# A feed-forward chunk's seven products: from five PSUM tiles to three banks, with five sums instead of seven

## The chip, the cores and the metric

The kernel runs on 1 core of one Trainium2 chip. The metric is device time in microseconds: the median of 3 runs, from the first to the last instruction of the program as the runs are timed.

## The reference

A block of a diffusion model, two layers deep, on one sequence of 512 tokens (1024 channels) with 256 context tokens. Each layer is: a feed-forward, four mixers side by side (attention in a window, a state space, grouped attention, neighbourhood attention), and a second feed-forward. Each of the three has a modulation before and after it and a norm behind it; in the last layer the context is dropped after the mixers. What the change touches is the feed-forward's first half:

```python
def swiglu(h, w_in, w_out):
    a, u = jnp.split(h @ w_in, 2, axis=-1)
    return (jax.nn.silu(a) * u) @ w_out
```

`h` has 768 tokens (512 and the context's 256) in three of the four feed-forwards and 512 in the last; `w_in` is 1024 x 5632, so that gate `a` and up `u` have 2816 columns each. All is float32.

## The kernel before, in words

**Arithmetic.** TensorE multiplies in a 32-bit format with a short mantissa (`float32r`). So each operand is split into two such parts, high and low, and `mm3` (L326 to L331) makes three matmuls of a product of two operands: high by high, low by high, high by low. A weight tile of 128 x 512 is split by `split_slot` (L322 a cast on ACT, L323 a subtraction on DVE), into one of six slots for `wh` and six for `wl`.

**Stages.** The program runs: input and modulations, feed-forward 1 of layer 0, mixers of layer 0 and their merge, feed-forward 2 of layer 0, feed-forward 1 of layer 1, mixers of layer 1 and their merge, feed-forward 2 of layer 1. A feed-forward takes its 2816 columns in 22 chunks of 128, in four to six parts; after each part the part's columns are multiplied with `w_out` and added to the residual (`branch_out`, with L468 and L470 on DVE reading and adding the sums; the last part has a form of its own). The first two chunks of each feed-forward are computed plainly (`first`), the other 20 by `winograd`, so it is called 80 times: 60 times with halves of 384 tokens, 20 times with halves of 256.

**A chunk.** Tokens and channels are halved, which makes a product of 2 x 2 blocks: A11, A12 (the first tokens) and A21, A22 (the second); B11 and B21 the gate's weights, B12 and B22 the up's. Winograd's scheme has seven block products in place of eight, with sums S1 to S4 of A's blocks, made once for each feed-forward, and T1 to T4 of B's, made for each chunk on POOL (`ffn_weights`, L605 to L613). With C11 and C21 the gate's results and C12 and C22 the up's:

```
U = A11 B11 + S2 T2      C11 = A11 B11 + A12 B21     C12 = U + S4 B22 + S1 T1
C21 = U + S3 T3 + A22 T4                             C22 = U + S3 T3 + S1 T1
```

Each block product is 4 channel chunks x 3 matmuls = 12 matmuls into one PSUM bank. `winograd` allots, for each chunk, three tiles of one bank (`psp`, two buffers) for A11 B11, A12 B21 and S1 T1, and two tiles of two banks (`ps2`, two buffers) for the others, in the order `one[:, 0]`, `two[:, 0]`, `one[:, 1]`, `two[:, 1]`. ACT copies the first product (L686); DVE adds each of the others to a running sum in SBUF (L688, L691, L692, L695, L696, L699, L700); ACT takes the silus (L689, L697), DVE multiplies (L701, L702), and `store` splits the result for the second half (L642 on ACT, L643 on DVE).

**Order.** The program names tiles, and a planner writes out each engine's order before the run: where it expects an instruction to wait, it puts a later one, of whatever stage, that it expects to be ready. On the chip each engine works through its list in that order. Waits on semaphores come from what is recorded of each tile's reads and writes, and a tile name with k buffers can be in use k times at once; `e0`, `e1`, `e2` and `ffg` have one buffer, `wraw` and `wrax` two each. All weights are loaded by SP's queue. `extra` (in the first and second feed-forward) is work on the modulations, one step ahead of a chunk's products and the rest in their midst; `behind` is work on the residual, put on POOL after a chunk's last weight sum.

Of the kernel before, what the change touches and what calls it, by code (L numbers as in the profile page):

```python
# [34 lines left out]
# columns of mix_w_in after the host's reordering (heads of aq and cq as 0, 2, 1, 3)  # L35
C_A, C_Z, C_XBC, C_C, C_D, C_BDT = 0, 512, 768, 1536, 2048, 2816

# columns of the constants
# [4 lines left out]
BY_SUM = (0, 4, 1, 5, 2, 6, 3, 7)  # channel chunks in the order of the feed-forward's sums  # L43
K_ID, K_SEL = K_N, K_N + P
GATES = (2, 5, 8)  # the modulations that multiply a branch
N_SLOTS = 2 * len(GATES)
K_ALL = K_SEL + 4 * N_SLOTS
# columns of the neighbourhood masks
# [4 lines left out]
def _constants():  # L53
# [19 lines left out]
    # sums of the four groups' rows of the modulations; for those that multiply a branch, half of it  # L73
    # where it is a feed-forward's, with the bias in rows 16 and on
# [17 lines left out]
def bcast(ap, n):  # L92
    """Repeats the elements of a [p, a, ...] operand n times along a new last dimension."""
    s = list(ap.shape)
    return ap.unsqueeze(len(s)).to_broadcast(s + [n])


def bcast1(ap, n):
    """Repeats a [p, ...] operand n times along a new first free dimension."""
    s = list(ap.shape)  # L100
    return ap.unsqueeze(1).to_broadcast([s[0], n] + s[1:])
# [12 lines left out]
def side_by_side(a, na, b, nb):  # L114
    """Runs two generators, of na and nb steps, so that both last as long."""
    i = j = 0
    while i < na or j < nb:
        if j >= nb or (i < na and i * nb <= j * na):
            next(a, None)
            i += 1  # L120
        else:
            next(b, None)
            j += 1
    for g in (a, b):
        for _ in g:
            raise AssertionError("more steps than told")


class Block:
    def __init__(self, ctx, tc, t, out):  # L130
# [7 lines left out]
        # the products' left operands, by channel, in two parts: inputs of the feed-forward and of  # L138
        # the mixers, then what the mixers give
# [25 lines left out]
    # ---------------------------------------------------------------- small parameters  # L165
    def turned(self, rows, tag):
        """Vectors cut in rows of 128, turned so that the channel is the partition."""
# [16 lines left out]
    def conditioning(self):  # L184
        """silu(c) and silu(c_ctx) as stationary operands: any two of 32 columns, the others zero."""
# [13 lines left out]
        # modulations by channel: layer, which of the nine, chunk, stream  # L199
# [39 lines left out]
    def ada_batch(self, l, ns, pool, at_once=()):  # L239
        """Two steps for each of these 512 columns of both streams' modulations; the last also places them: by  # L240
        channel (a shift and a scale's, in order), or, of what multiplies a branch, as rows in DRAM."""
# [48 lines left out]
    def mod_affine(self, l, i, halves=((0, KD),), into=None):  # L290
        """Scale and shift, by channel, of what follows norm i of layer l (i = -1: the input)."""
# [15 lines left out]
    # ---------------------------------------------------------------- weights and products  # L307
    def weights(self, src, shape):
        """Loads float32 weights, contraction chunks by columns, and splits each chunk into two float32r parts
        whose sum it is."""  # L310
# [6 lines left out]
    def split_slot(self, raw, slot=None):  # L317
        """The two parts of chunks [p, chunk, columns], in up to 512 columns."""
# [7 lines left out]
    def mm3(self, out, a, b, start, stop):  # L326
        """out += a'b with a and b given in two parts."""
        mm = self.nc.tensor.matmul
# [7 lines left out]
    # ---------------------------------------------------------------- residual stream  # L336
# [19 lines left out]
    def spill_res(self, n):  # L356
        """The residual's addend waits in DRAM while the mixers run."""
# [10 lines left out]
    def new_sums(self, pool, tiles):  # L368
        """Room for what the feed-forward's sums come from: act's value, by channel chunk."""
# [3 lines left out]
    def turn(self, tiles, aff, ks=range(KD)):  # L373
        """xT of these token tiles: turned, scaled and shifted by channel, split."""
# [15 lines left out]
    def rsqrt(self, tmp, x, n, mul=1.0):  # L390
        """(x * mul + EPS) ** -0.5 of n columns: a guess from the exponent, three Newton steps."""
# [11 lines left out]
    def stats(self, t, dh, tmp, gain=None):  # L403
        """Mean and variance of the token tile's half; after a pair's last, the pair normalised in place; with
        gain, each tile by itself, and the result of it put out."""
# [37 lines left out]
    def gain(self, l, i, tmp, tags):  # L443
        """A norm's gain and bias, on all partitions."""
# [5 lines left out]
    def rescale(self, l, i, tiles, tmp):  # L450
        """Normalised tiles times the gain and plus the bias, times alpha: the next residual's addend. One step
        for each tile."""
# [11 lines left out]
    def add(self, t, dh, acc, mrow, tmp, norm, gain=None):  # L464
        """512 columns of a product, times its modulation, to the residual."""
# [8 lines left out]
    def branch_out(self, l, i, tiles, steps, a_of, w_of, mrow, tmp, todo=None):  # L474
        """Adds a product, times its modulation, to the residual, 512 columns at a time; with todo, what
        comes of normalised tiles by number, the normalisation and that.

        steps: weight tiles' contraction chunks, in order; w_of(step, dh) loads one; a_of(k, t) the left
        operand's parts."""
# [34 lines left out]
    def follow(self, todo, upto, end):  # L514
        """After products of which end is the last: what follows token tiles up to this one."""
# [4 lines left out]
    def turns(self, aff, tmp, tiles):  # L520
        """What to do when a token tile is normalised."""
# [5 lines left out]
    def mod_rows(self, l, which, pool, streams):  # L527
        """The modulation that multiplies a branch, on all partitions."""
# [7 lines left out]
    # ---------------------------------------------------------------- feed-forward  # L536
    # The first product, of all tokens A and a chunk's gate and up weights B: with tokens and channels
    # halved, A21 the second tokens' first channels, and B12 the up weights' first channels, Winograd's seven
    # products:
    #   S1 = A21 + A22, S3 = A11 - A21, S2 = A22 - S3, S4 = A12 - S2  # L540
    #   T1 = B12 - B11, T3 = B22 - B12, T2 = T3 + B11, T4 = B21 - T2
    #   U = A11 B11 + S2 T2, C11 = A11 B11 + A12 B21, C12 = U + S4 B22 + S1 T1,
    #   C21 = U + S3 T3 + A22 T4, C22 = U + S3 T3 + S1 T1
    # The first chunks have the plain eight, while the sums come.
    def left(self, name):
        """Four channel chunks of half of the tokens, in two parts."""
# [6 lines left out]
    def sums(self, pool):  # L553
        """S2, S3 and S4, then S1 in A21's place: two steps of two channel chunks each, then one."""
# [32 lines left out]
    def ffn_weights(self, l, w_in, f, pool):  # L587
        """B11, B21, B22 and T1 .. T4 in two parts."""
# [12 lines left out]
        def put(name, src):  # L601
            w[name] = self.split_slot(src)
# [3 lines left out]
        tt(x[:, 0], x[:, 1], x[:, 0], op=ALU.add)  # L606
        put("B21", y[:, 0])
        put("T2", x[:, 0])
        put("B22", y[:, 1])
        put("T3", x[:, 1])  # L610
        tt(y[:, 0], y[:, 0], x[:, 0], op=ALU.subtract)
        put("T4", y[:, 0])
        last = tt(y[:, 1], y[:, 1], x[:, 0], op=ALU.subtract)  # L613
        put("T1", y[:, 1])
        return w, last

    def ffn(self, l, w_in, w_out, which, i, with_ctx, pool, after, parts, extra=None, final=False, early=()):
        """extra: work for the gaps, by feed-forward chunk. after: called when the next modulation is due,
        gives what to do by normalised tile. early: the first weights, if they are there."""
# [10 lines left out]
        def plain(gate_up, cols):  # L630
            """These tokens' products of one chunk, or (both at once) of its gate and up weights."""
# [916 lines left out]
```

## Time and profile before

| | |
|---|---|
| median of 3 runs | 3099.47 us (3094.49 to 3105.36) |
| span of the profiled execution | 3101.0 us (no other time of that execution is given) |
| busy: PE, DVE, ACT, POOL | 94%, 71%, 38%, 24% of the span |
| granted clock of PE, mean | 0.975 of full speed |
| instructions | 44820 |

How to read it: the profile is of one execution. PE is TensorE's matmuls, PEld its weight loads, DVE VectorE, ACT ScalarE, POOL GpSimd, SPq the queue from which the loads are issued. L330 is line 330 of the kernel. "tile <- tiles" says what an instruction writes and reads, by tile names without buffer numbers. Matmuls are pipelined: one of 384 columns is shown as 0.33 us, and the next in a row starts earlier than its end. Idle time of an engine, and what ended it, stands in brackets.

### The profile page before, as it was taken

To read this page: it belongs to the slowest core of one execution; us is meant where nothing else is said; L and a number is where in the kernel's file an instruction comes from. 1 tells how busy PE (TensorE), PEld (TensorE's weight loads), DVE (VectorE), ACT (ScalarE), POOL (GpSimd) and SP (SyncE) were. 2 spreads that over 40 slices of the span, in tenths; PEclk is the share of its full clock that TensorE was granted. 3 is DMA by queue.
4 is the path that set the end of the run, shared out by engine and by line. 5 is a ranking of instruction groups with operands and counts; after the bars stand their busy time and mean duration, and the time that the engine had idled before them with its cause. 6 is when DMAs were issued, how large, how long until landed. Compare 5 with 4: busy or idle time off the path is not lost.

```text
span 3101.0 us, 44820 instructions
## 1 busy us (share of the span) xinstructions
PE 2913.0 (94%) x16772; PEld 2485.0 (80%) x16772; DVE 2216.5 (71%) x4258; ACT 1172.8 (38%) x2153; POOL 734.8 (24%) x532
## 2 busy tenths in 40 slices
PE   8999999999999989999999799999989989889996
PEld 5888888778787767888888689998967777778886
DVE  5666667875757587666577976668786666888779
ACT  4333223342256443322233433332343356434333
POOL 1222212220112034221121531222150120234323
PEclk9999999999999999999999899999989999999998
DMA  6443334131133213544443122221222232233231
GB/s 207 156 143 125 111 105 136 60 106 41 42 85 61 89 55 89 177 133 132 129 156 118 60 68 68 68 82 49 68 93 67 70 80 64 75 115 88 82 96 69
DMA packets 319533, 296.17 MB, mean 96 GB/s; under 512 B 16631, under 2 KB 245071, under 8 KB 319059
## 3 DMA queue, kind: packets, MB, share of 16 engines
q1 hardware_dynamic: 318259, 290.80, 30.5%
q0 software_dynamic: 1056, 2.49, 0.4%
q8 instruction: 133, 2.18, 0.3%
q14 instruction: 85, 0.70, 0.1%
HBM read 270.52 MB, written 7.39 MB: 90 GB/s over the span
## 4 chain that ended last, share of the span: by engine, by line
PE 57%; DVE 17%; issue 3%; ACT 2%; DMA 1%; POOL 0%; DVEq 0%; SPq 0%; ACTq 0%; POOLq 0%
PE ps L329 8%; PE ps L331 8%; PE ps L330 8%; PE psp L329 7%; PE psp L330 7%; PE psp L331 7%; DVE wl L323 4%; PE ps L1025 2%; PE ps L1066 2%; PE psp L1082 2%; DVE actl L388 2%; DVE tmp L468 1%; PE ps L260 1%; DVE res L470 1%; ACT wh L322 1%
## 5 line engine op out<-in xcount | busy, mean ns | idle before, releaser
L323 DVE TENSOR_TENSOR wl<-wraw,wh 128x512 fp32r<-128x512 f32 x600 | 465.0, 782 | 341.7 <-ACT wh L322 336.2
L322 ACT CAST wh<-wraw 128x512 fp32r<-128x512 f32 x600 | 369.6, 620 | 897.3 <-PE ps L331 470.7
L329 PE MATMUL psp<-acth,wh 128*128 128x384 f32 (+2 forms) x1592 | 532.6, 335 | 24.1 <-DVE e L700 19.0
L330 PE MATMUL psp<-actl,wh 128*128 128x384 f32 (+2 forms) x1592 | 526.1, 331 | 2.7 <-DVE actl L388 2.7
L331 PE MATMUL psp<-acth,wl 128*128 128x384 f32 (+2 forms) x1592 | 524.6, 330 | 0.7 <-DVE wl L323 0.7
L329 PEld LDWEIGHTS psp<-acth,wh 128*128 128x128 f32 x1592 | 303.7, 191 | 72.9 <-ACT wh L322 49.0
L329 PE MATMUL ps<-S,wh 128*128 128x384 f32 (+1 forms) x960 | 315.2, 328 | 17.9 <-DVE ffg L638 7.7
L330 PEld LDWEIGHTS psp<-actl,wh 128*128 128x128 f32 x1592 | 303.5, 191 | 16.3 <-DVE actl L388 3.6
L331 PEld LDWEIGHTS psp<-acth,wl 128*128 128x128 f32 x1592 | 303.8, 191 | 12.8 <-issue 1.9
L331 PE MATMUL ps<-S,wl 128*128 128x384 f32 (+1 forms) x960 | 312.0, 325 | 1.2 <-DVE wl L323 1.2
L330 PE MATMUL ps<-S,wh 128*128 128x384 f32 (+1 forms) x960 | 312.0, 325 | 0.0
L461 POOL TENSOR_TENSOR res<-res,mrow 128x512 f32<-128x512 f32 x112 | 171.8, 1565 | 461.6 <-PE ps L383 340.8
L322 ACT CAST wh<-wrax 128x512 fp32r<-128x512 f32 x280 | 173.4, 620 | 271.6 <-PE ps L330 160.8
L323 DVE TENSOR_TENSOR wl<-wrax,wh 128x512 fp32r<-128x512 f32 x280 | 255.2, 918 | 7.2 <-ACT wh L322 6.2
L329 PE MATMUL ps<-wh,gTh 128*128 128x512 f32 x594 | 234.6, 395 | 8.3 <-DVE tmp L468 8.3
L331 PE MATMUL ps<-wh,gTl 128*128 128x512 f32 x594 | 233.4, 393 | 0.0
L330 PE MATMUL ps<-wl,gTh 128*128 128x512 f32 x594 | 233.1, 392 | 0.0
L330 PE MATMUL ps<-actl,wh 128*128 128x384 f32 (+2 forms) x568 | 202.5, 357 | 24.3 <-DVE actl L388 24.2
L329 PEld LDWEIGHTS ps<-S,wh 128*128 128x128 f32 x960 | 183.5, 191 | 42.8 <-ACT wh L322 26.7
L331 PE MATMUL ps<-acth,wl 128*128 128x384 f32 (+2 forms) x568 | 200.3, 353 | 8.1 <-DVE wl L323 8.1
L329 PE MATMUL ps<-acth,wh 128*128 128x384 f32 (+2 forms) x568 | 202.6, 358 | 3.7 <-ACT wh L322 2.3
L470 DVE TENSOR_TENSOR res<-res,tmp 128x512 f32<-128x512 f32 x268 | 190.9, 744 | 0.6
(369 smaller groups left out, 5727.4 us busy)
## 6 DMA issues: line engine op xcount, KB each, us to landing
araw<-in_ada_w_dram SPq DMA_DIRECT2D x128, 512.0 KB
wraw<-in_ffn_w_out_dram SPq DMA_DIRECT2D x88, 512.0 KB
wraw<-in_ffn_w_in_dram SPq DMA_DIRECT2D x160, 256.0 KB
wrax<-in_ffn_w_in_dram SPq DMA_DIRECT2D x160, 256.0 KB
wraw<-in_mix_w_in_dram SPq DMA_DIRECT2D x44, 512.0 KB
wraw<-in_ffn_w_in_dram SPq DMA_DIRECT2D x16, 512.0 KB
wraw<-in_mix_w_out_dram SPq DMA_DIRECT2D x16, 512.0 KB
mrow<-mrow SPq DMA_DIRECT2D x10, 512.0 KB
```

The source lines that it names most:

```text
L260: nc.tensor.matmul(ps[32 * g:32 * g + 32, :], lhsT=self.cs[:, k, c0:c0 + 32], rhs=w[:, k - kk, :], start=i == 0 and k < 4, stop=i == len(n ...
L322: self.nc.scalar.copy(h, raw)
L323: self.nc.vector.tensor_tensor(lo, raw, h.bitcast(F32), op=ALU.subtract)
L329: mm(out, lhsT=a[0], rhs=b[0], start=start, stop=False)
L330: mm(out, lhsT=a[0], rhs=b[1], start=False, stop=False)
L331: return mm(out, lhsT=a[1], rhs=b[0], start=False, stop=stop)
L388: nc.vector.tensor_tensor(l, y, h.bitcast(F32), op=ALU.subtract)
L461: nc.gpsimd.tensor_tensor(r, r, x[:, lo:hi], op=op)
L470: nc.vector.tensor_tensor(r, r, y, op=ALU.add)
L1025: nc.tensor.matmul(ps[:, at:at + hi - lo], lhsT=q, rhs=part[:, lo:hi], start=i == 0, stop=i == 1)
L1066: nc.tensor.transpose(pt[:, j * P:(j + 1) * P], p[:, a:a + P], self.ident)
L1082: nc.tensor.matmul(out[64 * a:64 * a + 64, :], lhsT=v[:, kt, vcol:vcol + 64], rhs=pT[:, i], start=i == 0, stop=i == len(order) - 1)
```

## The change

The comments and docstrings also go, in the whole file; that changes no instruction. Of the program, the order of the split weights and the body of `winograd` change. `mm3` and `product` get a flag `more`, with which a product's first matmul adds to what the bank holds. The products go to three banks: `a` (one bank of `psp`), `b` and `d` (the two banks of one `ps2` tile), in the order A11 B11 to a, S2 T2 to b, A12 B21 added to a, S3 T3 added to b, S1 T1 to d, A22 T4 added to b, S4 B22 added to d. A bank is read between two products that go to it.

```diff
-    def mm3(self, out, a, b, start, stop):
-        mm = self.nc.tensor.matmul
+    def mm3(self, out, a, b, start, stop, more=False):
+        mm = partial(self.nc.tensor.matmul, skip_group_check=more)
...
         tt(x[:, 0], x[:, 1], x[:, 0], op=ALU.add)
+        put("T2", x[:, 0])
         put("B21", y[:, 0])
-        put("T2", x[:, 0])
-        put("B22", y[:, 1])
         put("T3", x[:, 1])
         tt(y[:, 0], y[:, 0], x[:, 0], op=ALU.subtract)
+        last = tt(x[:, 0], y[:, 1], x[:, 0], op=ALU.subtract)
+        put("T1", x[:, 0])
         put("T4", y[:, 0])
-        last = tt(y[:, 1], y[:, 1], x[:, 0], op=ALU.subtract)
-        put("T1", y[:, 1])
+        put("B22", y[:, 1])
         return w, last
...
-        def product(out, w, a):
+        def product(out, w, a, more=False):
             for k, (wk, ak) in enumerate(zip(w, self.left(a))):
-                self.mm3(out, wk, ak, k == 0, k == 3)
+                self.mm3(out, wk, ak, k == 0 and not more, k == 3, more)
             return out
...
-            p1 = self.sb(pool, [n], "e0")
-            nc.scalar.copy(p1, product(self.psp()[:, :n], w["B11"], "A11"))
-            u, c12 = (self.sb(pool, [n], t) for t in ("e1", "e2"))
-            add(g[:, :n], product(self.psp()[:, :n], w["B21"], "A12"), p1)
-            nc.scalar.activation(g[:, :n], g[:, :n], AF.Silu)
-            one, two = self.ps2()[:, :, :n], self.ps2()[:, :, :n]
-            add(u, product(one[:, 0], w["T2"], "S2"), p1)
-            add(c12, product(two[:, 0], w["B22"], "S4"), u)
+            p1, u, v = (self.sb(pool, [n], t) for t in ("e0", "e1", "e2"))
+            a, two = self.psp()[:, :n], self.ps2()[:, :, :n]
+            b, d = two[:, 0], two[:, 1]
+            nc.scalar.copy(p1, product(a, w["B11"], "A11"))
+            add(u, product(b, w["T2"], "S2"), p1)
+            nc.scalar.activation(g[:, :n], product(a, w["B21"], "A12", True), AF.Silu)
             for e in rest:
                 e()
-            add(u, product(one[:, 1], w["T3"], "S3"), u)
-            add(p1, product(two[:, 1], w["T4"], "A22"), u)
-            nc.scalar.activation(g[:, n:], p1, AF.Silu)
-            p5 = product(self.psp()[:, :n], w["T1"], "S1")
-            add(c12, p5, c12)
-            add(u, p5, u)
-            mult(g[:, :n], g[:, :n], c12)
-            mult(g[:, n:], g[:, n:], u)
+            add(v, product(b, w["T3"], "S3", True), p1)
+            add(g[:, n:], product(d, w["T1"], "S1"), v)
+            add(v, product(b, w["T4"], "A22", True), p1)
+            nc.scalar.activation(v, v, AF.Silu)
+            mult(g[:, n:], g[:, n:], v)
+            add(u, product(d, w["B22"], "S4", True), u)
+            mult(g[:, :n], g[:, :n], u)
```

## Rows read from the trace of the kernel before

**Rows 1.** The page, part 1: busy us (share of the span) xinstructions.

```profile
PE 2913.0 (94%) x16772; PEld 2485.0 (80%) x16772; DVE 2216.5 (71%) x4258; ACT 1172.8 (38%) x2153; POOL 734.8 (24%) x532
```

**Rows 2.** Windows: third and fourth feed-forward. Stretch, length, busy, clock, DMA.

```profile
core 0: us, PE busy (x) PEld busy (x) DVE busy (x) ACT busy (x) POOL busy (x), PEclk, DMA share, GB/s
...
1775.00:2225.00 450.00, 444.05 (x2312) 411.30 (x2313) 323.54 (x500) 154.03 (x259) 111.24 (x80) 1.00 0.23 69
2715.00:3062.00 347.00, 316.57 (x2124) 291.54 (x2123) 284.62 (x432) 142.40 (x263) 114.06 (x83) 0.98 0.31 93
```

**Rows 3.** Windows: one chunk of 384 tokens, one of 256; columns as in rows 2.

```profile
1854.70:1869.30 14.60, 14.60 (x87) 14.60 (x86) 11.18 (x18) 6.51 (x11) 5.24 (x4) 1.00 0.24 72
...
2947.30:2959.17 11.87, 10.49 (x87) 10.18 (x85) 11.68 (x18) 5.85 (x11) 5.57 (x4) 1.00 0.33 87
```

**Rows 4.** Waits of PE, whole run: us in total, times, longest us.

```profile
PE psp L329 <- DVE e L700: 21.7, 15, 2.8
...
PE ps L329 <- DVE tmp L468: 8.3, 13, 1.1
...
PE ps L329 <- DVE e L691: 6.8, 6, 2.2
...
PE ps L383 <- ACT S L385: 3.9, 8, 1.0
```

**Rows 5.** Timeline of PE, last feed-forward: start, us, engine, line, tiles, shapes [idle].

```profile
2921.64 0.36 PE L329 MATMUL psp<-acth,wh 128*128 128x256 f32 x1 [2.79 <-DVE e L700]
...
2955.88 0.28 PE L330 MATMUL psp<-actl,wh 128*128 128x256 f32 x1
2956.00 0.28 PE L331 MATMUL psp<-acth,wl 128*128 128x256 f32 x1
2957.66 0.36 PE L329 MATMUL psp<-acth,wh 128*128 128x256 f32 x1 [1.38 <-DVE e L700]
```

**Rows 6.** Timeline of DVE and POOL in a chunk of the last feed-forward.

```profile
2948.60 0.68 DVE L323 TENSOR_TENSOR wl<-wraw,wh 128x512 fp32r<-128x512 f32 x1
...
2949.41 1.29 POOL L606 TENSOR_TENSOR wraw<-wraw 128x512 f32<-128x512 f32 x1 [4.97 <-DVE wl L323]
...
2949.68 1.58 DVE L323 TENSOR_TENSOR wl<-wraw,wh 128x512 fp32r<-128x512 f32 x1
...
2956.77 0.41 DVE L699 TENSOR_TENSOR e<-psp,e 128x256 f32<-128x256 f32 x1
2957.11 0.41 DVE L700 TENSOR_TENSOR e<-psp,e 128x256 f32<-128x256 f32 x1
```

**Rows 7.** Timeline: T2's last matmul, the next product's first, and L691, a chunk of 384.

```profile
1842.08 0.33 PE L331 MATMUL ps<-S,wl 128*128 128x384 f32 x1
...
1842.25 0.33 PE L329 MATMUL ps<-S,wh 128*128 128x384 f32 x1
...
1842.45 0.56 DVE L691 TENSOR_TENSOR e<-ps,e 128x384 f32<-128x384 f32 x1 [0.23 <-PE ps L331]
```

**Rows 8.** Timeline: a chunk in which L691 runs late; T3 starts at 1795.39.

```profile
1794.10 0.34 PE L331 MATMUL ps<-S,wl 128*128 128x384 f32 x1
...
1794.69 0.55 DVE L691 TENSOR_TENSOR e<-ps,e 128x384 f32<-128x384 f32 x1
...
1795.39 0.41 PE L329 MATMUL ps<-S,wh 128*128 128x384 f32 x1 [0.95 <-DVE e L691]
```

**Rows 9.** Timeline of PE: transposes (L383) with a later product's matmuls between them.

```profile
1707.86 0.66 PE L383 MATMUL ps<-ident,res 128*128 128x128 f32 x4 [0.44 <-ACT S L385]
1708.82 0.50 PE L330 MATMUL ps<-actl,wh 128*128 128x512 f32 x1 [0.30 <-DVE actl L388]
1709.15 0.60 PE L383 MATMUL ps<-ident,res 128*128 128x128 f32 x4
1709.51 0.48 PE L331 MATMUL ps<-acth,wl 128*128 128x512 f32 x1
```

**Rows 10.** Windows: the stretch behind the gap at 2921.64; columns as in rows 2.

```profile
2922.00:2926.00 4.00, 4.00 (x23) 4.00 (x23) 2.99 (x6) 1.93 (x4) 0.74 (x1) 0.57 0.78 232
```

## The prediction

> **What bounds the kernel now.** I read the page's busy times first: PE is busy 94% of the span, DVE 71%, ACT 38%, so the PE stream sets the end nearly everywhere [rows 1]. Then the same numbers stage by stage, over the four feed-forwards, which is where the changed code runs. In the third one (384 tokens to a half) PE is busy 444 of 450 us and DVE 324; in the last one (256 to a half) PE is busy only 317 of 347 and DVE 285 [rows 2]. So only the last leaves PE idle for long: 30.4 us. One clean chunk of each says it more sharply: a chunk of 384 takes 14.60 us with PE busy for all of them and DVE for 11.18; a chunk of 256 takes 11.87 us with DVE busy for 11.68 and PE for 10.49 [rows 3]. The first kind is bound by PE, the second by DVE.
>
> The waits of PE come next. The longest one of the chunks is on L700, 21.7 us in 15 waits, all of it in the last feed-forward; L691 holds PE for 6.8 us in 6 waits over the whole run [rows 4]. L700 is the second sum after product T1. The next chunk's second product takes that PSUM buffer, since three of the seven products share two single banks. The typical wait is 1.38 us [rows 5].
>
> Where DVE's time goes in that chunk: a split of a weight takes 0.68 us alone and 1.58 us when a POOL subtraction (here L606, 1.29 us) overlaps it, whereas a sum that reads PSUM takes 0.41 us, and the next one starts 0.34 us later [rows 6].
>
> **The change part by part.** Seven products stay seven, of 12 matmuls each. The seven sums become five; the two mults, two silus and one copy stay. DVE so loses 2 x 80 sums: 60 chunks x 2 at 0.56 us [rows 7] and 20 x 2 at 0.41 [rows 6], some 84 us of busy time. Beside PE in the 60 chunks that are PE-bound this is worth nothing, because DVE has 3.4 us to spare there [rows 3]. In the 20 DVE-bound chunks two sums at 0.34 us apiece are 0.68 us off the period, 14 us in all. Bounds: 0 if PE becomes late for another reason, 30 if all of that stage's idle time goes [rows 2]. I take 14, the sums' own length, because the splits and the POOL work beside them stay.
>
> The L700 wait itself goes: a chunk now takes one single-bank tile, and the two buffers alternate between chunks. What is late next is the point of the forecast. Products now return to a bank that DVE or ACT has just read: the copy of P1 before B21, u before T3, v before T4, the C22 sum before B22. By banks each of these has one product between, 12 x 0.17 = 2.08 us [rows 7], and a read is over 1.08 us after the last matmul began (below), so by banks nothing stops.
>
> But the trace says that a product waits for more than its own bank. T3 of the kernel before writes one[:, 1]; L691 reads one[:, 0], the other bank of that tile. When L691 ran late, T3's first matmul stood idle for 0.95 us and began 0.15 us after L691's end at 1795.24 [rows 8]; the list of waits names L691 as what ended a wait six times [rows 4], and nothing that L691 writes goes into T3. So what a product waits for is kept per tile, not per bank. Before, that was harmless, as consecutive products went to one, two, one, two. In the changed kernel b and d are the two banks of one tile, and after the third product the order is T3 (b), T1 (d), T4 (b), B22 (d). T1 then has to wait for the sum that reads T3's result, T4 for the one that reads T1's, B22 for the one that reads T4's: three turns in every chunk in which the read comes directly between two products, 240 in all.
>
> The price of a turn with nothing to cover it: the last matmul of a product starts at 1842.08, DVE's sum at 1842.45 (0.37 later), it lasts 0.56, and PE goes on 0.15 after its end [rows 7, 8]; that makes 1.08 us from start to start, against 0.17 for the next matmul in a row, so 0.91 us. For 256 tokens the sum is 0.41 and the step 0.12 [rows 5, 6]: 0.81 us. All uncovered: 60 x 3 x 0.91 + 20 x 3 x 0.81 = 213 us.
>
> They are not all uncovered. The order of an engine is written out beforehand, and where a wait is foreseen, later work is put into it: while the transposes L383 wait for ACT's L385, matmuls of the product after them stand between them [rows 9]. In a turn the next chunk's B11 and T2 can stand, as their weights are split ahead (wh and wl have six slots) and their banks are the other buffers: 0.91 us is five matmuls of 0.17. What such filling leaves open is not shown for this place. From below it is nothing, and not less, as a product can't start sooner than right behind the last. From above it is the whole 0.91. The nearest rows are those interleaved steps: four in a row have 0.44, 0.30, 0 and 0 us of idle time before them, 0.19 on average [rows 9]; the unfilled waits on L385 and L468 come to 3.9 / 8 = 0.49 and 8.3 / 13 = 0.64 us apiece [rows 4]. I take 0.19, since the filled steps resemble a turn most: 240 x 0.19 = 45 us.
>
> The order of the weights changes with that of the products: T2 comes second and so needs POOL's L605 and L606 before any other split but B11's. In mid-stage the six slots let the splits run five products, some 10 us, ahead, which hides POOL's 1.29 us [rows 6]; at the first chunk of a feed-forward and after each output stage nothing does, and T2, in a two-bank tile, also comes one product sooner after the output stage's reads. Bounds: 0, and one product (2.08 us) at each of some 20 such places, 42 us; I take 6, since L468, what those reads are, now costs PE 8.3 us in all [rows 4].
>
> The rest at nothing, both ways: a silu that reads PSUM rather than SBUF (ACT is busy 6.5 us of a chunk's 14.6 [rows 3]; if that cover went, at most 80 times the 0.56 us of a sum of that size, 45 us); T1's difference written over another tile, the same four POOL operations in the same order, with as many DMAs on SP's queue; and the modulation steps called one product earlier in the chunk. DVE's sums wait for products as before; behind a waiting sum stand splits, which have five products of room.
>
> **The sum.** 45 - 14 + 6 = +37 us on the profiled execution's span of 3101.0, so 3138; the runs' median is 3099.47, 1.5 us below that span, so 3137 as the runs count.
>
> **Rule against row.** Rows 8 show a product waiting for a read of another bank. The Trainium skill, "PSUM — Partial Sum Buffer", section "Terms", says that two engines must be kept apart when they are on the same bank and quadrant at once; other banks are free. By that rule the turns would cost nothing, and it is the first rival below. This trace does not agree with it as the whole of what this kernel waits for.
>
> **The rivals.**
> 1. Banks, not tiles, or turns wholly filled. T1, T4 and B22 start without delay, the L700 wait goes, and the last feed-forward becomes as long as its PE work or as DVE's shortened work: -14 to -30 us, I take -22: 3078. For it: in the clean chunk T3, one product behind L691, never stands [rows 3, 7], and filling exists [rows 9]. Against it: rows 8. Chance 0.25.
> 2. The filling covers turns but for the odd one, and its rest equals the 14 us saved: 3100, within 9 us either way. Chance 0.13.
> 3. Turns uncovered: no work is put in, or what is put in stands behind the same wait. 213 - 14 + 6 = +205: 3305. It decides from a remainder of about 0.8 us a turn on. For it: L700's 1.38 us waits of the last feed-forward were not filled [rows 5]. Against: rows 9. Chance 0.09.
> 4. The gaps bring the clock down. After one gap of 2.79 us [rows 5] the granted clock was 0.57 on average over 4 us, most of them at 1.2 GHz, the lower of its two levels [rows 10]: 4 x 0.43 = 1.7 us lost. Once a chunk that is 1.7 x 80 = 136 us on top of 37: 3274. Against it: the clock was 1.00 through a chunk with a gap of 1.38 us [rows 3, 5], longer than any turn's. Chance 0.03. The Trainium skill, "TensorE: Matmul & The Clock Gate", section "A second HAM failure mode: psum-queue depth-cycling", says that short pauses at every change of PSUM bank make the clock swing; this trace doesn't agree for pauses of that length.
>
> The forecast, slower by turns partly filled, has 0.50; its own range is 0.05 to 0.45 us a turn, 3105 to 3200.
>
> **How the numbers follow.** What a measurement of this kernel can tell from no change is about 0.3%, 9 us. Faster is rival 1: 0.25. Within is rival 2: 0.13. Slower is the forecast with rivals 3 and 4: 0.62. The range goes from 3078 (the middle of rival 1, half of which, 0.12, lies below) to 3200; above that lie rivals 3 and 4 and with them 0.12 less what of rival 3 is half filled, about 0.08.
>
> **What would show it.** Right: waits of PE on the three sums that read b and d in the chunks of 384, where now there is none; a PE order in which matmuls of the next chunk's B11 (single bank) stand between T3 and T1; a chunk longer than 14.6 us; no wait of PE on a single bank's sum in the last feed-forward; DVE's busy time some 84 us lower. Wrong: chunks of 384 still at 14.6 us with T1 starting 0.17 us after T3's last matmul (banks count), or PE idle close to 0.9 us at each turn (nothing was filled), or the clock below 1.00 within such chunks.

## The result, and the profile after

The changed kernel takes 3190.82 us (median of 4 runs, 3188.66 to 3195.13) where the kernel before takes 3098.93: a ratio of 1.0296 (95% interval 1.0279 to 1.0312), 92 us slower. Forecast was +37. The direction held, the size did not.

The page's first part, columns as in [rows 1]:

```profile
PE 2967.7 (93%) x16772; PEld 2485.2 (78%) x16772; DVE 2093.2 (66%) x4098; ACT 1156.3 (36%) x2153; POOL 737.1 (23%) x532
```

DVE lost 123 us of busy time: 82 for the two sums a chunk (84 were forecast) and 50 on splits (those from `wrax` went from 918 to 783 ns on average), while other work took 8 longer. PE has the same 16772 instructions and is busy 55 us longer; its idle time grew by 38 us. So more than half of the loss does not show as a wait (a pause shows in part as busy time: see no_fill below). To see where it lies, each feed-forward is taken from its first copy of P1 to its twentieth. Windows of those stretches, first the kernel before (first, third and fourth feed-forward), columns as in [rows 2]:

```profile
86.50:553.10 466.60, 461.56 (x2459) 398.92 (x2458) 310.32 (x496) 150.20 (x250) 101.78 (x76) 1.00 0.40 125
...
1776.60:2209.40 432.80, 427.21 (x2226) 395.42 (x2226) 311.69 (x480) 145.69 (x247) 109.96 (x80) 1.00 0.22 68
2718.70:3050.00 331.30, 301.57 (x2020) 277.95 (x2019) 272.23 (x410) 133.52 (x248) 110.97 (x81) 0.98 0.31 93
```

and the changed one (third, fourth and first):

```profile
1821.50:2275.60 454.10, 436.93 (x2227) 396.26 (x2228) 288.29 (x438) 138.94 (x244) 111.81 (x80) 0.99 0.22 66
2783.60:3142.00 358.40, 315.18 (x2030) 284.10 (x2029) 218.80 (x369) 128.47 (x248) 114.42 (x82) 0.97 0.29 86
87.60:578.00 490.40, 483.14 (x2472) 403.45 (x2473) 288.62 (x460) 145.65 (x250) 101.10 (x76) 0.99 0.39 119
```

The four stretches grew by 24, 21, 21 and 27 us, which is all of it. In the first feed-forward PE is busy for 21.6 of the 23.8 us more; in the last, where DVE was the bound and should have been relieved, DVE is busy 53 us less and the stretch is the one that lost most.

**What PE was busy with.** The chunks of the first two feed-forwards also carry the modulation's matmuls (L260): four of 32 columns each, a quad, with the weights on four groups of PE's columns. Groups of PE, the kernel before and then the changed one:

```profile
L260 PE MATMUL ps<-araw,cs 128*32 128x512 f32 x512 | 71.9, 605 | 0.1
```

```profile
L260 PE MATMUL ps<-araw,cs 128*32 128x512 f32 x512 | 100.2, 612 | 0.0
```

The same 512 records, 28.3 us more. The timeline of PE shows why. The kernel before (a quad is 8 records, since each of its matmuls is two):

```profile
1266.11 1.06 PE L260 MATMUL ps<-araw,cs 128*32 128x512 f32 x8
1267.10 0.45 PE L329 MATMUL ps<-S,wh 128*128 128x384 f32 x1
```

and the changed one:

```profile
1278.39 1.04 PE L260 MATMUL ps<-araw,cs 128*32 128x512 f32 x2
1279.37 0.45 PE L329 MATMUL ps<-acth,wh 128*128 128x384 f32 x1
...
1281.68 1.06 PE L260 MATMUL ps<-araw,cs 128*32 128x512 f32 x6
1282.67 0.44 PE L331 MATMUL psp<-acth,wl 128*128 128x384 f32 x1
```

A whole quad takes 0.99 us from start to the next start; one matmul of it takes 0.98, the other three 0.99. The planner put one into one turn and three into the next. So the filling itself costs a quad's time, and that shows as busy PE. In the order written out for PE, 30 of the 64 quads are broken so, where 2 were before. (The Trainium skill, "TensorE: Matmul & The Clock Gate", section "Part 3: Packing small matmuls — row/col tiling", gives the span of matmuls packed side by side as that of one plus some 4 ns for each further one; these rows agree.) The other 26 us of PE's longer busy time are not taken apart here.

**What PE waited for.** The longest waits on the chunks' lines, PE, whole run, columns as in [rows 4]; L700 has no counterpart among them any more:

```profile
PE psp L329 <- ACT e L691: 29.8, 10, 10.7
...
PE ps L329 <- DVE e L698: 10.8, 4, 4.2
PE ps L329 <- DVE e L692: 9.8, 14, 3.8
PE ps L329 <- DVE ffg L697: 9.2, 11, 1.6
...
PE ps L329 <- DVE e L696: 8.0, 12, 1.2
```

L696 to L698 are the three turns. L691 is ACT's copy of P1, on which B21 waits, as it is added to the bank that the copy reads. A turn of 4.2 us is far over any price of the forecast, and the timeline around it shows a chain over four engines (last feed-forward; start, us, engine, line, tiles, idle time):

```profile
2885.12 1.30 POOL L605 TENSOR_TENSOR wraw<-wraw,wraw 128x512 f32<-128x512 f32 x1 [3.55 <-DMA wraw<-in_ffn_w_in_dram]
...
2886.38 1.26 POOL L610 TENSOR_TENSOR wrax<-wrax,wrax 128x512 f32<-128x512 f32 x1
2887.72 1.26 POOL L611 TENSOR_TENSOR wrax<-wrax,wrax 128x512 f32<-128x512 f32 x1
2889.01 1.14 ACT L322 CAST wh<-wrax 128x512 fp32r<-128x512 f32 x2 [4.91 <-POOL wrax L611]
2889.66 0.69 DVE L323 TENSOR_TENSOR wl<-wrax,wh 128x512 fp32r<-128x512 f32 x1 [4.83 <-ACT wh L322]
2890.27 0.42 DVE L698 TENSOR_TENSOR e<-ps,e 128x256 f32<-128x256 f32 x1
...
2890.74 0.58 PE L329 MATMUL ps<-S,wh 128*128 128x256 f32 x1 [4.24 <-DVE e L698]
```

POOL makes T1's weights of the next chunk (L611). ACT's cast of them waits 4.91 us, DVE's split waits for the cast, and behind the split in DVE's list stands the sum L698, whose product was long done. PE needs that sum for its turn. The weights themselves are not wanted yet; what is late is what stands behind them in line. (The Trainium skill, "PSUM — Partial Sum Buffer", section "Engine vs sequencer instructions", calls the queues of these three engines strict FIFO; the rows agree.)

POOL was late in this place for the same reason. Ahead of L610 in its list stands L605 of the chunk after that one, which waits 3.55 us for its load, while the split of B21 that L610 needs was over at 2883.55. So some 2.8 of the 4.24 us begin with a load, and no run here moved it. Over the whole run L605 waits for loads hardly longer than with the old order of the weights (456 us against 447 in turns_old, below), so what the new order changed is mostly what stands behind it. Without turns these waits do grow, from 379 us in old_weights to 487 in own_tiles; what that costs is open.

The waits of ACT's casts for POOL, whole run, the kernel before and the changed one:

```profile
ACT wh L322 <- POOL wrax L606: 28.2, 18, 2.3
ACT wh L322 <- POOL wraw L606: 27.9, 13, 4.6
ACT wh L322 <- POOL wraw L611: 3.8, 1, 3.8
ACT wh L322 <- POOL wraw L613: 3.0, 1, 3.0
```

```profile
ACT wh L322 <- POOL wraw L606: 114.8, 40, 6.9
ACT wh L322 <- POOL wraw L611: 50.3, 13, 4.9
ACT wh L322 <- POOL wrax L606: 37.3, 31, 4.3
ACT wh L322 <- POOL wrax L611: 35.1, 11, 4.9
```

63 us became 238.

### The profile page after: what moved, and what is told of

It is laid out like the page before. It is cut to its first block, busy times and chain, and to the rows that moved or that the text cites. A ratio compares the mean times of both kernels' runs of the same rounds, so it can differ in the third digit from the quotient of the medians.

```text
span 3193.4 us, 44148 instructions
## 1 busy us (share of the span) xinstructions
PE 2967.7 (93%) x16772; PEld 2485.2 (78%) x16772; DVE 2093.2 (66%) x4098; ACT 1156.3 (36%) x2153; POOL 737.1 (23%) x532
## 5 line engine op out<-in xcount | busy, mean ns | idle before, releaser
L329 PE MATMUL psp<-acth,wh 128*128 128x256 f32 (+2 forms) x1272 | 428.9, 338 | 40.8 <-ACT e L691 29.8
L330 PE MATMUL psp<-actl,wh 128*128 128x256 f32 (+2 forms) x1272 | 425.1, 334 | 3.8 <-DVE actl L388 3.8
L331 PE MATMUL psp<-acth,wl 128*128 128x256 f32 (+2 forms) x1272 | 424.8, 334 | 0.7 <-DVE wl L323 0.7
L329 PE MATMUL ps<-acth,wh 128*128 128x384 f32 (+2 forms) x888 | 316.9, 358 | 21.4 <-DVE ffg L697 9.2
L330 PE MATMUL ps<-actl,wh 128*128 128x384 f32 (+2 forms) x888 | 309.4, 348 | 24.2 <-DVE actl L388 24.0
L331 PE MATMUL ps<-acth,wl 128*128 128x384 f32 (+2 forms) x888 | 306.3, 345 | 8.1 <-DVE wl L323 8.1
L329 PEld LDWEIGHTS psp<-acth,wh 128*128 128x128 f32 x1272 | 245.0, 193 | 72.3 <-ACT e L691 32.7
L331 PEld LDWEIGHTS psp<-acth,wl 128*128 128x128 f32 x1272 | 244.7, 192 | 26.8 <-issue 16.1
L330 PEld LDWEIGHTS psp<-actl,wh 128*128 128x128 f32 x1272 | 244.8, 193 | 16.9 <-DVE actl L388 4.5
L329 PEld LDWEIGHTS ps<-acth,wh 128*128 128x128 f32 x888 | 174.4, 197 | 74.8 <-DVE ffg L697 31.1
```

Source lines behind the costliest of these rows:

```text
L329: mm(out, lhsT=a[0], rhs=b[0], start=start, stop=False)
L330: mm(out, lhsT=a[0], rhs=b[1], start=False, stop=False)
L331: return mm(out, lhsT=a[1], rhs=b[0], start=False, stop=stop)
```

## The experiments

Two suspects came first: the turns (theory A), and something else of the change. Ratios are to the kernel before, which was run again beside each group of runs (medians of 3099.7 to 3101.0 us), with their 95% intervals.

**own_tiles**: no turns.

```diff
-            a, two = self.psp()[:, :n], self.ps2()[:, :, :n]
-            b, d = two[:, 0], two[:, 1]
+            a, b, d = self.psp()[:, :n], self.ps2()[:, 0, :n], self.ps2()[:, 0, :n]
```

> The changed kernel with b and d in two PSUM tiles of their own instead of the two banks of one; order of products, five sums and weights stay. Theory A (the waits are kept per tile, so T1, T4 and B22 wait for the sum just before, and gaps, fillings and broken quads of the modulation all follow from that): the waits on the sums L696, L697 and L698 go, the modulation's matmuls run in whole quads again, chunks of 384 are back at 14.56 (third feed-forward) and 17.0 us (second), chunks of 256 at 11.3 to 11.9: 3075 to 3100, I say 3080. Rival B (adding to a bank that is not cleared, T2 as the second product, or P1's single buffer costs the time, not the tile): chunks stay above 15 us, 3150 to 3190.

3167.08 us (1.0213; 1.0198 to 1.0229). The waits on the three turns go and quads are whole (62 of 64), yet only 24 of the 92 us go with them. PE now waits 67.4 us, 26 times, on the copy of P1. The time lies in the rival's range, which names three causes at once; the turns are real, but most of the loss is not theirs.

**before_paired**: the turns alone, in the seven-sum kernel.

```diff
-            add(c12, product(two[:, 0], w["B22"], "S4"), u)
+            add(c12, product(one[:, 1], w["B22"], "S4"), u)
...
-            add(u, product(one[:, 1], w["T3"], "S3"), u)
+            add(u, product(two[:, 0], w["T3"], "S3"), u)
```

> The kernel before, seven sums and its order of products and weights, with the four products of the two-bank tiles handed out T2, B22 to the one tile and T3, T4 to the other, so that two turns a chunk (B22 after T2's sum, T4 after T3's) come up within a tile. Theory A (turns by tile): 160 turns and quads of the modulation broken by filling, 3130 to 3170, I say 3150. Rival B (banks, or the five-sum scheme itself, set the time): within 9 us of 3099.

3144.94 us (1.0153; 1.0130 to 1.0176). Same sums, same banks, same orders; only which bank lies in which tile. B22 and T4 each take the other bank of a tile whose sum is due just before: PE's waits on T3's sum (L695), of which the kernel before has none, are 9.1 us in 15 waits; those on T2's sum (L691) went from 6.8 to 16.6. 27 quads are broken, and L260 is busy 97.0 us. The waits are kept per tile, as theory A has it.

**quads_kept**: one modulation step is held between T3 and T1, the other behind B22, so that a quad stays together (the edit is a `with self.tc.issue_after(...)` around each quad and around T1's product).

```diff
...
-            for e in rest:
-                e()
             add(v, product(b, w["T3"], "S3", True), p1)
-            add(g[:, n:], product(d, w["T1"], "S1"), v)
+            self.front, self.quad = self.end, None
+            for e in rest:
+                e()
+            self.front = None
+            with self.tc.issue_after(self.quad.ins) if self.quad else nullcontext():
+                s1 = product(d, w["T1"], "S1")
+            add(g[:, n:], s1, v)
...
```

> The changed kernel with its turns, but the matmuls of a modulation step (four that run side by side in four groups of 32 columns) are held together: one step stands in the turn between T3 and T1, the other behind B22. Theory A2 (of what the first two feed-forwards lost, most is broken quads: a fourth of a quad takes 0.98 us like the whole, 30 times, and the rest is the turn's remainder): the first feed-forward's stretch of winograd chunks falls from 490 to some 472, the second's from 499 to some 482, 3150 to 3165 in all. Rival C (the turn costs its full length whatever stands in it): within 9 us of 3191.

3163.16 us (1.0206; 1.0189 to 1.0223). The first two stretches fall from 490 and 499 to 471 and 484 us, the others stay. As A2 has it: 28 us were broken quads.

**no_fill**: the first two products of a chunk behind the last of the chunk before (`self.end` is the last matmul written so far).

```diff
-            nc.scalar.copy(p1, product(a, w["B11"], "A11"))
-            add(u, product(b, w["T2"], "S2"), p1)
+            with self.tc.issue_after(self.end.ins) if self.end else nullcontext():
+                s0 = product(a, w["B11"], "A11")
+            nc.scalar.copy(p1, s0)
+            with self.tc.issue_after(self.end.ins):
+                s2 = product(b, w["T2"], "S2")
+            add(u, s2, p1)
```

> The changed kernel with the first two products of a chunk held behind the last of the chunk before, so that nothing of the next chunk can stand in a turn. Theory A (a turn costs 0.91 us at 384 tokens and 0.81 at 256 when nothing covers it): chunks of the third feed-forward at 14.56 + 3 x 0.91 = 17.3 us against some 15.3 of the changed kernel, of the fourth at about 13.5; 3250 to 3300, I say 3270. Rival C (filling is worth nothing, the turns cost what they cost in the changed kernel anyway): within 20 us of 3191.

3275.74 us (1.0565; 1.0549 to 1.0581). In the midst of its parts the third feed-forward's chunks take 17.36 to 17.42 us, from copy to copy, where the kernel before has 14.56; 14.56 + 3 x 0.91 is 17.3. The three turns of one, timeline of PE (the matmuls' lines are two further down than in the changed kernel, the sums' six):

```profile
1932.16 0.45 PE L331 MATMUL ps<-acth,wh 128*128 128x384 f32 x1 [0.65 <-DVE e L702]
...
1935.19 0.44 PE L331 MATMUL ps<-acth,wh 128*128 128x384 f32 x1 [0.65 <-DVE ffg L703]
...
1938.22 0.44 PE L331 MATMUL ps<-S,wh 128*128 128x384 f32 x1 [0.65 <-DVE e L704]
```

The idle time shown is 0.65, not 0.91. Around the first, 0.17 us of the pause stand under the modelled end of the matmul before it (started at 1931.17, shown as 0.34 us), and 0.11 under the one behind it (the next starts at 1932.44, 0.28 us later where 0.17 is usual): 0.93 in all. The price of a turn was right, and so was that filling pays for most of it.

Then what is left in own_tiles. Theory D: the copy of P1, one product ahead of B21. Theory E: the weights, late by their new order. All four have tiles of their own.

**six_sums**: B21 into a single bank of its own.

```diff
-            nc.scalar.activation(g[:, :n], product(a, w["B21"], "A12", True), AF.Silu)
+            add(g[:, :n], product(self.psp()[:, :n], w["B21"], "A12"), p1)
+            nc.scalar.activation(g[:, :n], g[:, :n], AF.Silu)
```

> b and d in tiles of their own, and the second product into the single bank (A12 B21) put into another single bank, with a sixth sum on DVE that adds P1; weights and order as in the changed kernel. Theory D (with the turns gone, what is left in own_tiles is PE waiting for ACT's copy of P1, since B21 is added to the bank that the copy reads, one product later, and the copy stands in ACT's queue behind casts that wait for POOL): the 67 us of waits on the copy go, 3080 to 3110, I say 3095. Rival E (the wait on the copy only names the place; the weights come late because of their new order, and PE stands for that elsewhere): 3150 to 3170.

3154.34 us (1.0172; 1.0155 to 1.0189): 13 of 67 us. The wait moved to the next sum: 55.0 us on L691, which here is T2's sum. Theory E's figure.

**spread**: B21 as the fifth product, T1 as the third, its weights earlier.

```diff
-            nc.scalar.activation(g[:, :n], product(a, w["B21"], "A12", True), AF.Silu)
...
+            s1 = product(d, w["T1"], "S1")
             add(v, product(b, w["T3"], "S3", True), p1)
-            add(g[:, n:], product(d, w["T1"], "S1"), v)
+            add(g[:, n:], s1, v)
+            nc.scalar.activation(g[:, :n], product(a, w["B21"], "A12", True), AF.Silu)
```

> Tiles of their own and five sums, but the products in the order B11 (a), T2 (b), T1 (d), T3 (b), B21 (a), T4 (b), B22 (d), so that three products stand between B11 and the B21 that is added to its bank; T1's weights are made earlier for it. Theory D: the copy of P1 has 6.2 us rather than 2.1 at 384 tokens, 4.3 rather than 1.4 at 256, so the waits on it go nearly wholly: 3075 to 3110, I say 3090. Rival E (late weights): as late as own_tiles or later, 3150 to 3180.

3226.17 us (1.0403; 1.0383 to 1.0422), worse than either theory said. The copy's waits are gone from the top of the list, but 41.9 us of waits for the modulation's loads came, so this run speaks against D without measuring E.

**dve_copy**: `nc.vector.tensor_copy(p1, ...)` in place of `nc.scalar.copy`.

> Tiles of their own and five sums in the changed kernel's order, with P1 copied by DVE in place of ACT. Theory D, if it is ACT's queue with its casts waiting for POOL that makes the copy late: DVE's queue has splits that wait for these same casts, so some of the wait stays, and 80 copies of 0.4 to 0.56 us come to DVE: 3120 to 3165, I say 3140. Rival E: as own_tiles, within 9 us of 3167.

3176.52 us (1.0246; 1.0231 to 1.0261). No gain: PE still waits 50.9 us, 24 times, for the copy, now on DVE, whose splits wait for the same casts (569 us in all). That these casts are why it stays late is argued, not tested.

**old_weights**: `ffn_weights` as it was before.

```diff
-        put("T2", x[:, 0])
         put("B21", y[:, 0])
+        put("T2", x[:, 0])
+        put("B22", y[:, 1])
         put("T3", x[:, 1])
         tt(y[:, 0], y[:, 0], x[:, 0], op=ALU.subtract)
-        last = tt(x[:, 0], y[:, 1], x[:, 0], op=ALU.subtract)
-        put("T1", x[:, 0])
         put("T4", y[:, 0])
-        put("B22", y[:, 1])
+        last = tt(y[:, 1], y[:, 1], x[:, 0], op=ALU.subtract)
+        put("T1", y[:, 1])
```

> Tiles of their own, five sums and the changed kernel's order of products, with the weights made and split in the order of the kernel before (B21 before T2, T1 last). Theory D: the copy stays one product ahead of B21 and behind the same casts, so most of own_tiles' loss stays, 3145 to 3180. Rival E (the order of the weights makes them late): most of the 67 us goes, 3090 to 3115.

3113.13 us (1.0041; 1.0026 to 1.0056). Theory D falls, E stands: 54 of own_tiles' 67 us are the order of the weights. It is not the clock, whose mean is 0.973 in both traces. The products keep the changed kernel's order, so it is the order in which the weights are made and split, not the order of their use. ACT waits 42.5 us for POOL here.

**turns_old**: the same edit in the changed kernel itself, turns and all.

> The changed kernel, b and d in one two-bank tile, with the weights made and split in the order of the kernel before. Theory A+F (the turns and the order of the weights are two separate costs): it keeps the turns and loses the late weights, some 47 us in own_tiles' trace, of which 33 lie in the last feed-forward, where turns and late weights partly hide each other: 3140 to 3165, I say 3155, and 30 broken quads. Rival (the turns are only slow because the weights are late): 3113, as with tiles of their own.

3135.81 us (1.0113; 1.0098 to 1.0128): 55 us less than the changed kernel, and 4 under the range expected. So there are two separate costs. The window of the last feed-forward's stretch, columns as above:

```profile
2764.10:3083.10 319.00, 304.88 (x2020) 275.84 (x2019) 230.85 (x368) 129.65 (x246) 117.28 (x81) 0.99 0.32 96
```

There lie 39 us of the difference (319.0 against 358.4).

**t2_late** and **t1_last**: own_tiles with one half of the new order each put back: T2 behind B21 again, or T4 and then T1 last again, with one difference of POOL ahead of each (B22's split then comes ahead of T3's, as in the kernel before).

> Tiles of their own; of the new order of the weights only T2 is put back behind B21; T1 ahead of T4 and B22 stays. Theory F1 (T1's cast, which stands behind two POOL sums one after the other, blocks ACT's queue, and P1's copy behind it: that gap was 4.2 us in a chunk of the last feed-forward of own_tiles): most of the loss stays, 3150 to 3170. Theory F2 (T2 second is what is late: it needs two POOL sums 1 product after B11): most goes, 3115 to 3130.

> Tiles of their own; the new order keeps T2 as the second product's weights, and T4, then T1 come last with one POOL sum ahead of each, as in the kernel before (B22's split moves ahead of T3's). Theory F1: most of the loss goes, 3115 to 3135, the last feed-forward near 330 us. Theory F2: it stays, 3150 to 3170.

3121.96 us (1.0069; 1.0054 to 1.0084) and 3129.00 (1.0088; 1.0071 to 1.0105). Neither theory alone: either half put back returns most (45 and 38 us, both together 54). By the program, the two halves lie in one chain. With T2 second, its cast waits for POOL and B21's cast stands behind it; POOL's L610 needs B21's split, L611 needs L610, and T1's cast needs L611. ACT's waits for POOL are 322 us in own_tiles, 173 in t1_last, 89 in t2_late.

**six_old**: old_weights and six_sums together.

> Tiles of their own, the weights' order of the kernel before, and B21 in a single bank of its own with a sixth sum. Theory: no turn, no late weights, no wait of B21 for the copy of P1 (47.8 us of waits in old_weights, most of them at the start of each feed-forward and of each of its parts); the last feed-forward some 7 us shorter than before by one sum less: 3085 to 3099, I say 3092, the first version under the kernel before. Rival: the copy's wait moves to the sum (as in six_sums), 3105 to 3115.

3098.47 us (0.9994; 0.9984 to 1.0003): not to be told from the kernel before. Against old_weights, B21 on the bank of P1 costs 15 us, net of the sixth sum.

What was open then: whether the weights' order costs as much in the seven-sum form, by which chain, and whether quads are what is left of turns_old.

**seven_new**: the kernel before with its sums and tiles, weights and products in the new order (added lines of `winograd`, where a product moved).

```diff
+            add(u, product(one[:, 0], w["T2"], "S2"), p1)
             add(g[:, :n], product(self.psp()[:, :n], w["B21"], "A12"), p1)
...
+            add(v, product(two[:, 0], w["T3"], "S3"), u)
+            p5 = product(self.psp()[:, :n], w["T1"], "S1")
...
+            add(v, product(one[:, 1], w["T4"], "A22"), v)
...
+            add(u, product(two[:, 1], w["B22"], "S4"), u)
```

> The kernel before with seven sums, five PSUM tiles and no turn, but with weights and products in the order of the changed kernel (B11, T2, B21, T3, T1, T4, B22). Theory G (the order of the weights is a cost of its own, whatever the banks and sums are): some 45 to 65 us over 3100, most of it in the last feed-forward; I say 3150. Rival (the late weights hurt only because B21 is added to the bank that ACT copies): 3095 to 3110.

3147.30 us (1.0148; 1.0130 to 1.0166). No shared bank, no turn, no fewer sums: the order of weights and products alone costs 46 us, 28 of them in the last feed-forward's stretch (359.4 against 331.3).

**t1_dve**: T1's difference on DVE, in own_tiles.

```diff
-        tt(y[:, 0], y[:, 0], x[:, 0], op=ALU.subtract)
-        last = tt(x[:, 0], y[:, 1], x[:, 0], op=ALU.subtract)
+        last = tt(y[:, 0], y[:, 0], x[:, 0], op=ALU.subtract)
+        nc.vector.tensor_tensor(x[:, 0], y[:, 1], x[:, 0], op=ALU.subtract)
```

> own_tiles with T1's difference made by DVE instead of POOL, the orders unchanged. Theory G2 (in the new order T1's cast, the fifth of a chunk, stands behind all four POOL sums, each waiting for the split before it, and ACT's queue stands behind that cast): one sum of 1.3 to 1.7 us less in that chain, so that half or more of the 54 us between own_tiles and old_weights goes: 3115 to 3140, I say 3130. Rival (the order of the casts itself, or the raw buffers coming free later, sets it): within 9 us of 3167, or later by DVE's added 80 x 0.7 us in the last feed-forward.

3142.09 us (1.0130; 1.0112 to 1.0149): 25 of 54 us back, a little less than expected. ACT's waits on T1's difference (L611) fall from 165 us, on POOL, to 99 us, on DVE, where it still waits for L610; those on T2's sum (L606) stay, with 173 us. So T1's link is a part of the cause; the exact share of each link stays open.

**quads_old**: turns_old with quads_kept.

> turns_old (two banks of one tile, the weights' order of the kernel before) with the modulation's quads held together as in quads_kept. Theory A2: 30 broken quads of 0.98 us were nearly all that the turns cost in the first two feed-forwards: 3100 to 3115, I say 3107. Rival C (the turns cost their time whatever stands in them): 3127 to 3145.

3113.23 us (1.0038; 1.0027 to 1.0050): 23 us less than turns_old, and as fast as old_weights, which has no turns. L260 is busy 72.3 us again. So, filled with products of the next chunk and with whole quads, 240 turns cost nothing that these times can tell. In the midst of a part, from copy to copy, most chunks of 384 in the third feed-forward take 14.72 us against 14.56 in old_weights, which makes 0.05 us a turn; most of 256 take 11.15 to 11.7 against 11.63.

**mixed**: `if with_ctx:` the kernel before's body, otherwise turns_old's.

> The kernel before in the three feed-forwards of 384 tokens to a half, and turns_old's form (three banks, five sums, the weights' order of the kernel before) in the last one, with 256. Theory: the last feed-forward's stretch of chunks takes 319 us instead of 331, as in turns_old's trace, because there DVE is the bound and two sums a chunk less count; nothing else changes: 3083 to 3093, I say 3088. Rival (the gain of that stretch is given back by the start or the tail): within 9 us of 3100.

3087.97 us (0.9957; 0.9941 to 0.9972): 13 us faster than the kernel before, the best version found. The window of the last feed-forward's stretch, columns as above:

```profile
2717.10:3035.50 318.40, 303.29 (x2020) 274.47 (x2019) 233.16 (x368) 129.78 (x246) 117.55 (x81) 0.99 0.32 97
```

318.4 us for 331.3, with three banks, five sums and all three turns in every chunk.

## Why the prediction was wrong

The step that failed is "The order of the weights ... Bounds: 0, and one product (2.08 us) at each of some 20 such places, 42 us; I take 6". It measured 55 us (the changed kernel against turns_old), over its upper bound, and 46 to 54 in the other pairs (seven_new, own_tiles against old_weights). The working asked when PE would want T2 and found five products of room. It didn't ask what stands behind a cast that waits for POOL: in ACT's list the copy of P1 and the silus, in DVE's list, behind the split that needs the cast, the sums. And it priced T2 alone: that T1's difference is wanted ahead of T4 and B22 it put at nothing, as "the same four POOL operations in the same order", and either half put back returned most of the loss (t2_late, t1_last). For DVE it said that "behind a waiting sum stand splits, which have five products of room"; the wait came the other way round, a split waiting with a sum behind it. And it placed the cost at starts and output stages; 28 of seven_new's 46 us and 39 of the changed kernel's 55 lie in the last feed-forward, where a chunk has the same weights to make in less time (11.87 us against 14.60 [rows 3]); that this is why is not tested.

The others, in the order of the sum:

- **Turns, +45.** That the waits go by tile, and the price of 0.91 us, held (before_paired for the first, no_fill for the second). Of the 45 us 23 to 28 came, and for another reason: they were put as 0.19 us of idle time at each of 240 turns. In fact a filled turn costs next to nothing (quads_old against old_weights), and what came is what the planner filled it with, broken quads in the first two feed-forwards. [Rows 9] were the wrong neighbour: there the filler was work that took as long elsewhere.
- **DVE's two sums less, -14.** It measured -13 (mixed), net of the turns and of the copy's waits in that stage. In the changed kernel itself it was buried under the weights.
- **B21 on the bank of P1, taken as stopping nothing "by banks".** It costs 15 us (old_weights against six_old), since the copy can be late in ACT's list though the bank's own timing leaves a product of room. PE's longest waits for it are at the starts of feed-forwards (2.8, 6.9 and 9.2 us in old_weights). In most chunks of the last one it waits 1.3 us, and there six_old's sixth sum costs as much (stretches of 325.4 and 323.9 us).
- **The sum.** With its 6 replaced by 55 it gives 37 + 49 = 86 us, against 92. That the rest fits so well is luck: the turns, put at 45, gave 23, and B21's copy, put at nothing, gave 15. Step by step the runs go -2 (six_old), +15 (old_weights), +23 (turns_old) and +55 (the changed kernel), 91 in all.
- **The rivals.** Banks, not tiles (3078): fell with before_paired. Uncovered turns (3305): no_fill is that case, at 3276. The clock: behind the gap of 4.24 us above it was lower for a while, a window of the changed kernel shows:

```profile
2891.00:2904.00 13.00, 12.25 (x80) 11.92 (x80) 8.57 (x14) 4.30 (x9) 4.66 (x4) 0.79 0.29 82
```

That is 2.7 us lost (13 x 0.21). Over the whole run the mean clock is 0.970 against 0.975, which withholds 96 us against 78. So at most 18 of the 92 us are the clock's, and less as far as PE was idle then. Pauses of the length of a turn alone didn't bring it down: from 1930.0 to 1964.8 us of no_fill, two chunks with six such pauses, it was 1.00.

## What to carry to other kernels

When an edit reorders who needs a slow helper engine, list for each in-order engine, the slow one too, what stands behind the instruction that will now wait; the due time of its own result says little. A gap that a planner fills is not free if the filler shared the engine side by side with its neighbours: look at busy time for the same instruction count, not only at idle time. Two banks of one tile are one thing to the waits; take the tiles apart, or make sure that whole work is there to fill.

## What the runs showed that was not expected

One of four 32-column matmuls that run side by side takes as long as all four (0.98 and 0.99 us), so that breaking them shows as 28 us of busy PE. Two edits that each cost 9 to 16 us alone beside the old order (t1_last and t2_late against old_weights) cost 54 together. And of a change that loses 3% over the kernel, the banks and sums gain 13 us when they are kept to the stage that DVE bounds and the weights keep their order.
